# A decoder layer on one core: wider moving operands in up and query/key, an eleventh pair in down, another order at both ends

## The chip, the cores and the metric

The kernel runs on one core of one Trainium2 chip. The metric is the device time of one execution in microseconds; for the kernel before it is the median of three runs.

## What is computed

One decoder layer on x of 256 rows by 2048 columns, all in float32:

```python
h   = rmsnorm(x)                 # 2048 columns, gain
qkv = h @ w_in                   # 2048 x 6144: 16 heads of 128
# heads 0-7 stick-breaking attention, heads 8-15 rotary + dilated windows
mix = concat(head_rmsnorm(heads)) @ w_out
x   = x + rmsnorm(mix)
u   = causal_conv3(rmsnorm(x) @ w_up)        # 2048 x 11008
x   = x + rmsnorm((gelu(gate) * val) @ w_down)   # 5504 x 2048
```

## The kernel before

Matmuls run in fp32r. To keep float32's accuracy every operand is split in a high part (a copy, rounded) and a low part (the rest), and each product is three matmuls: high by high, high by low, low by high. A weight tile of 128 x 1024 (`raw`, 5 buffers, one DMA of 512 KB on SP's queue) becomes `wh` by ACT's cast (`high`, L86) and `wl` by DVE's subtraction (`low`, L91), 4 buffers each.

The work is a list of **chunks**, each one weight block of 2048 columns: 16 for the values (`v`), 32 for query and key (`qk`, one head's query or key each), 16 for the output projection (`out`), 86 for `up` (43 tiles of 128 gate columns, 43 of value columns, by turns). After each chunk the attention of some heads moves on by one step. In `v`, `out` and the down stage the weights are the moving operand, 512 columns at a time (`mm_moving`, L116 to L132). In `qk` and `up` the weights are stationary and the activations move, 256 columns (the sequence) at a time: `mm_stationary` (L94) multiplies each of the 16 blocks of `wh` with the high activations `hT0` (L100) and with the low ones `hT1` (L101), into the same 256 columns of PSUM, and then each block of `wl` with `hT0` (L104): 48 matmuls in a chunk. The first two up chunks go through `mm_stationary_late` (L106), which keeps that order of its own. `convolved` (L425) scales an up result by the row norm on DVE, straight from PSUM (L430), adds the three-tap convolution, and gives gate times value to `yt` or `yp`.

The **down stage** (class `Down`, L460) multiplies with w_down in two column halves (`cp` 0 and 1). Its 43 row tiles are units: a single ("one") has 4 products of 128x512; two tiles that form a pair take 7 products in place of 8, by sums of blocks (T13, T24 on DVE, L517 to L519; Rb, Ra). A pair needs four `wh` and four `wl`. `_down_plan` (L39) sets the order: 10 pairs with two singles behind each. `prepare` runs four units ahead of `multiply`. The sums T13 and T24 and the gain `gbc` lie in `spare`, the results in `fg`; `spare` takes the place of `hT1` and `fg` that of `hT0` after the last up chunk. `combine` (L540) and `close` (L550) bring the PSUM banks together when a half is done; `close` ends in a square sum on ACT, and in a gain product (`take`, L378) on DVE.

At the end of half 1 three singles are held back and multiplied bank by bank, first the banks of output rows 0 to 127, then those of rows 128 to 255, so that the norm of the first rows (`mean`, `newton`) and its four output steps (`put`, L577, and the output DMA) run beside the matmuls of the second. `put` scales, adds the residual and issues the DMA.

```python
T.matmul(ps, ws, hi[:, k, :], start=(k == 0), stop=False)      # L100
T.matmul(ps, ws, lo[:, k, :], start=False, stop=False)         # L101
...
spare = cpool.tile([P, 2 * D], F32, tag="hT1", name="spare")   # L762
```

A scheduler orders the instructions of each engine, apart from stretches marked to stay as written; each engine and each DMA queue then runs its list in order.

Of the kernel before, what the change touches and what calls it, by code (L numbers as in the profile page):

```python
# [33 lines left out]
NPAIR = 10  # L34
PAIRS = [(4 * m, 4 * m + 1) for m in range(NPAIR)]
# [14 lines left out]
def layer_kernel(ctx: ExitStack, tc: tile.TileContext, a, out: bass.AP):  # L50
# [135 lines left out]
    hT = [cpool.tile([P, KT, S], F32R, tag=f"hT{i}", name=f"hT{i}") for i in range(2)]  # L186
# [12 lines left out]
    def load_x(lo, hi):  # L199
        nc.sync.dma_start(xt[:, lo:hi, :], a["xT"][:, lo * S:hi * S].rearrange("p (k s) -> p k s", k=hi - lo))  # L200
# [27 lines left out]
    nc.scalar.dma_start(ident, a["cst"][:, C_ID:C_END])  # L228

    negones = cpool.tile([P, P], F32, name="negones")  # L230
# [102 lines left out]
    def dilated_head(h, ps):  # L333
        rot = apool.tile([P, 2, S], F32, tag="t2", name="rot", bufs=3)
        A.copy(rot[0:64], ps[64:128])
        A.copy(rot[64:128], ps[0:64])
        qk = apool.tile([P, 2, S], F32, tag="qk", name="qk", bufs=3)
        V.tensor_tensor(qk, ps, cosR, op=ALU.mult)
# [502 lines left out]
```

## Time and profile before

| | |
|---|---|
| median of 3 runs | 1142.37 us (1142.11 to 1142.76) |
| the profiled execution | 1142.97 us, of which the span is 1141.2 us |
| PE busy | 1119.8 us, 98% of the span, 7708 matmuls |
| DVE, ACT, POOL busy | 815.2, 625.8 and 2.0 us |
| the chain that ended last | 95% PE |
| granted TensorE clock | 0.998 of full |
| DMA | 217 MB, 190 GB/s on the mean |

The page gives each engine's busy time in the span, then the chain of work that ended last. An engine's busy share is an average over stages with different limits. For matmuls the recorded length is the latency of one; since they are pipelined, what one costs is the distance from its start to the next one's.

### The profile page before, as it was taken

The numbers are of one execution on the slowest core, as the hardware profiler recorded it, in microseconds if no ns is written. First come the engines' busy times: TensorE is split into PE (matmuls) and PEld (weight loads), VectorE is DVE, ScalarE is ACT, GpSimd is POOL, SyncE is SP. The second block draws the span as 40 slices with busy tenths as digits, with TensorE's granted clock in tenths as the row PEclk, the third lists the DMA queues.
The fourth block names the chain that finished last, engine by engine and source line by source line (L and its number), as shares of the span: only waits on it lengthen the run. The fifth ranks groups of instructions, "written<-read, shape, count | busy, mean of one in ns | idle before, by whom it ended". The sixth has DMA issues, their size and how long they took to land.

```text
span 1141.2 us, 19401 instructions
## 1 busy us (share of the span) xinstructions
PE 1119.8 (98%) x7708; PEld 1034.4 (91%) x7708; DVE 815.2 (71%) x1218; ACT 625.8 (55%) x919; POOL 2.0 (0%) x8
## 2 busy tenths in 40 slices
PE   7999999999999989999999999999999999999996
PEld 5998999989988889999999999999999988877884
DVE  6655565665655488777777777776777788898887
ACT  7555555555644376555555555555555555555653
POOL 0000000000000000000000000000000000000000
PEclk9999999999999999999999999999999999999999
DMA  9755545555545556555555555555555556645565
GB/s 341 268 197 166 180 153 166 167 163 173 167 164 187 182 192 201 186 188 185 187 186 187 184 187 184 190 185 184 186 185 185 185 191 216 207 161 205 206 199 184
DMA packets 60138, 217.08 MB, mean 190 GB/s; under 512 B 6800, under 2 KB 7696, under 8 KB 59280
## 3 DMA queue, kind: packets, MB, share of 16 engines
q1 hardware_dynamic: 59904, 215.78, 57.2%
q8 instruction: 60, 0.98, 0.3%
q14 instruction: 30, 0.25, 0.1%
q10 hardware_dynamic: 144, 0.07, 0.0%
HBM read 211.63 MB, written 4.19 MB: 189 GB/s over the span
## 4 chain that ended last, share of the span: by engine, by line
PE 95%; DVE 2%; ACT 1%; DMA 1%; issue 0%; DVEq 0%; SPq 0%; ACTq 0%
PE mmu L101 14%; PE mmu L104 14%; PE mmu L100 14%; PE p L536 6%; PE p L537 6%; PE p L535 6%; PE mmqk L100 5%; PE mmqk L104 5%; PE mmqk L101 5%; PE mmo L127 3%; PE mmo L130 3%; PE mmo L126 3%; PE mmv L126 2%; PE mmv L127 2%; PE mmv L130 2%; DMA mg<-in_xT 1%
## 5 line engine op out<-in xcount | busy, mean ns | idle before, releaser
L86 ACT CAST wh<-raw 128x1024 fp32r<-128x1024 f32 (+1 forms) x388 | 395.7, 1023 | 354.0 <-PE mmu L101 173.3
L91 DVE TENSOR_TENSOR wl<-raw,wh 128x1024 fp32r<-128x1024 f32 (+1 forms) x388 | 458.5, 1189 | 170.2 <-ACT wh L86 169.0
L100 PE MATMUL mmu<-hT,wh 128*128 128x256 f32 x1344 | 326.2, 281 | 0.2 <-ACT wh L86 0.2
L101 PE MATMUL mmu<-hT,wh 128*128 128x256 f32 x1344 | 325.8, 281 | 0.0
L100 PEld LDWEIGHTS mmu<-hT,wh 128*128 128x128 f32 x1344 | 253.9, 189 | 0.4 <-ACT wh L86 0.4
L101 PEld LDWEIGHTS mmu<-hT,wh 128*128 128x128 f32 x1344 | 252.6, 188 | 0.0
L104 PE MATMUL mmu<-hT,wl 128*128 128x256 f32 x1344 | 186.4, 281 | 0.0
L104 PEld LDWEIGHTS mmu<-hT,wl 128*128 128x128 f32 x1344 | 170.4, 188 | 0.0
L100 PE MATMUL mmqk<-hT,wh 128*128 128x256 f32 x512 | 126.8, 286 | 0.0
L101 PE MATMUL mmqk<-hT,wh 128*128 128x256 f32 x512 | 124.0, 281 | 0.0
L430 DVE TENSOR_TENSOR u<-mmu,r2B 128x256 f32<-128x256 f32 x86 | 36.4, 424 | 97.2 <-PE mmu L104 97.1
L101 PEld LDWEIGHTS mmqk<-hT,wh 128*128 128x128 f32 x512 | 96.6, 189 | 0.2
L100 PEld LDWEIGHTS mmqk<-hT,wh 128*128 128x128 f32 x512 | 96.4, 188 | 0.2
L86 ACT CAST wh<-spare 128x1024 fp32r<-128x1024 f32 x40 | 42.1, 1051 | 67.4 <-DVE spare L517 58.6
L536 PE MATMUL p<-wh,yt 128*128 128x512 f32 x184 | 73.4, 399 | 0.0
L535 PE MATMUL p<-wh,yt 128*128 128x512 f32 x184 | 72.5, 394 | 0.0
L537 PE MATMUL p<-wl,yt 128*128 128x512 f32 x184 | 71.8, 393 | 0.2 <-DVE wl L91 0.2
L104 PE MATMUL mmqk<-hT,wl 128*128 128x256 f32 x512 | 71.0, 281 | 0.0
L432 ACT ACTIVATE cv<-u,par 128x256 f32<-128x256 f32 x86 | 51.7, 602 | 27.6 <-DVE u L430 27.6
L104 PEld LDWEIGHTS mmqk<-hT,wl 128*128 128x128 f32 x512 | 65.1, 188 | 0.0
L126 PE MATMUL mmv<-wh,hT 128*128 128x512 f32 x128 | 52.6, 411 | 6.7 <-ACT hT L206 5.4
L536 PE MATMUL p<-wh,yp 128*128 128x512 f32 x140 | 55.8, 399 | 0.0
(165 smaller groups left out, 1343.6 us busy)
## 6 DMA issues: line engine op xcount, KB each, us to landing
raw<-in_w_up SPq DMA_DIRECT2D x172, 512.0 KB, 4.6
raw<-in_w_dn SPq DMA_DIRECT2D x86, 512.0 KB, 4.1
raw<-in_w_qk SPq DMA_DIRECT2D x64, 512.0 KB, 3.6
raw<-in_w_o SPq DMA_DIRECT2D x32, 512.0 KB, 3.6
raw<-in_w_v SPq DMA_DIRECT2D x30, 512.0 KB, 3.8
x<-in_x SPq DMA_DIRECT2D x2, 1024.0 KB, 8.8
x_kept<-x SPq DMA_DIRECT2D x2, 1024.0 KB, 4.1
x1b<-x_kept SPq DMA_DIRECT2D x4, 512.0 KB, 4.9
```

What stands on the lines that cost most here:

```text
L86: pin(A.copy(wh, raw))
L91: pin(V.tensor_tensor(wl, raw, wh.bitcast(F32), op=ALU.subtract))
L100: T.matmul(ps, ws, hi[:, k, :], start=(k == 0), stop=False)
L101: T.matmul(ps, ws, lo[:, k, :], start=False, stop=False)
L104: T.matmul(ps, wl[:, j * P:(j + 1) * P], hi[:, k, :], start=False, stop=(k == KT - 1))
L126: T.matmul(ps[t], hi[:, k, tc_], ws, start=(first and i == 0 and j == 0), stop=False)
L127: T.matmul(ps[t], lo[:, k, tc_], ws, start=False, stop=False)
L130: T.matmul(ps[t], hi[:, k, tc_], wl[:, j * 512:(j + 1) * 512], start=False, stop=(last and i == len(parts) - 1 and j == n - 1))
L432: A.activation(cv, u, AF.Identity, scale=cw(2), bias=par[:, P_CB + f:P_CB + f + 1])
L535: T.matmul(ps, hi, wh[:, cs], start=(cp, bank) not in self.begun, stop=False)
L536: T.matmul(ps, lo, wh[:, cs], start=False, stop=False)
L537: T.matmul(ps, hi, wl[:, cs], start=False, stop=self.left[cp, bank] == 0)
```

## The change

In `qk` and `up` the high and low activations now lie in one tile `hT2`, side by side for each block, and one matmul with 512 moving columns takes the place of L100 and L101; its two halves land side by side in one bank, and the low weights still take 256 columns (L104). The two halves are added afterwards: ACT copies one out of PSUM, DVE adds the other (`both` in up, the same two steps in qk, where the sum then lies in SBUF before the head's first step). The down stage forms 11 pairs and 21 singles in place of 10 and 23; singles are spread evenly between pairs, except that 4 remain for the end of each half. The gain products of half 0 are no longer run at the change of halves but one behind each of the first singles of half 1. `gbc` is multiplied by -0.5 once, and `take` becomes a plain product; three of the four of half 1, and half of the last, run on POOL. At the end the last bank is split in two halves of 256 columns, and the output steps have other widths. At the start the x tiles and the gain come through ACT's queue, eight matmuls on zeros run first, and the first chunk's weights come in three pieces in place of four. In `qk` and `first_norm`, tiles move between pools; the other edits not shown here give the same steps new operands.

```diff
-NPAIR = 10
-PAIRS = [(4 * m, 4 * m + 1) for m in range(NPAIR)]
+NPAIR = 11
+HELD = 4
+PAIRS = [(FT // NPAIR * m, FT // NPAIR * m + 1) for m in range(NPAIR)]
...
     plan = [("one", left.pop(0)) for _ in range(0 if cp else 2)]
+    spread = len(left) - HELD
     for m in range(NPAIR):
         plan.append(("pair", m))
-        plan += [("one", left.pop(0)) for _ in range(2 if cp or m < NPAIR - 1 else 0)]
+        plan += [("one", left.pop(0)) for _ in range((m + 1) * spread // NPAIR - m * spread // NPAIR)]
     return plan + [("one", k) for k in left]
...
-    def mm_stationary(ps, parts, hi, lo):
+    def mm_stationary(ps, parts, h):
...
-                ws = wh[:, j * P:(j + 1) * P]
-                T.matmul(ps, ws, hi[:, k, :], start=(k == 0), stop=False)
-                T.matmul(ps, ws, lo[:, k, :], start=False, stop=False)
+                T.matmul(ps, wh[:, j * P:(j + 1) * P], h[:, k, :, :], start=(k == 0), stop=False, skip_group_check=True)
             for j in range(8):
                 k = 8 * i + j
-                T.matmul(ps, wl[:, j * P:(j + 1) * P], hi[:, k, :], start=False, stop=(k == KT - 1))
+                T.matmul(ps[:, 0, :], wl[:, j * P:(j + 1) * P], h[:, k, 0, :], start=False, stop=(k == KT - 1), skip_group_check=True)
...
+    def both(ps, pool, name):
+
+        half = pool.tile([P, S], F32, tag="half", name="half", bufs=1)
+        A.copy(half, ps[:, 1, :])
+        u = pool.tile([P, S], F32, tag=name, name=name)
+        V.tensor_tensor(u, ps[:, 0, :], half, op=ALU.add)
+        return u
...
-    hT = [cpool.tile([P, KT, S], F32R, tag=f"hT{i}", name=f"hT{i}") for i in range(2)]
+    hT2 = cpool.tile([P, KT, 2, S], F32R, tag="hT", name="hT")
+    hT = [hT2[:, :, i, :] for i in range(2)]
...
-    for k in range(4):
-        raws[0] += load(chunks[0][3][:, k * 512:(k + 1) * 512], 512)
-        load_x(k, k + 1)
-        if k == 0:
-            nc.sync.dma_start(gpre, a["par"][:, P_PRE:P_PRE + KT])
-        split_x(k, k + 1)
-        parts_of[0] += split(raws[0][k:k + 1])
+    nc.scalar.dma_start(gpre, a["par"][:, P_PRE:P_PRE + KT])
+    warm = cpool.tile([P, 512], BF16, name="warm")
+    V.memset(warm, 0.0)
+    idle = ps_at.tile([P, 512], F32, tag="at", name="idle")
+    for _ in range(8):
+        T.matmul(idle, warm[:, 0:P], warm, start=True, stop=True)
+    for lo, hi in ((0, 1), (1, 2), (2, 4)):
+        raws[0] += load(chunks[0][3][:, lo * 512:hi * 512], (hi - lo) * 512)
+        load_x(lo, hi, nc.scalar)
...
+            split_x(lo, hi)
+            parts_of[0] += split(raws[0][-1:])
+    nc.scalar.dma_start(ident, a["cst"][:, C_ID:C_END])
...
-        u = phB.tile([P, S], F32, tag="u", name="u")
-        V.tensor_tensor(u, ps, r2B, op=ALU.mult)
+        u = both(ps, phB, "u")
+        V.tensor_tensor(u, u, r2B, op=ALU.mult)
...
-                        t13, t24 = spare[:, D:D + HALF], spare[:, D + HALF:]
+                        t13, t24 = room[:, 3, 0:HALF], room[:, 3, HALF:]
...
-            rows.squares(dst, t, col)
-            return lambda: rows.take(dst, t, col)
+            rows.squares(dst, t, col + (1 if lo else 0))
+            return lambda eng: eng.tensor_tensor(dst, dst, gbc[:, col * 512 + lo:col * 512 + hi], op=ALU.mult)
...
+                    if later and self.units[u][1] == "one":
+                        later.pop(0)(V)
                 if cp == 0:
-                    for b in (4, 3, 2, 8):
-                        self.close(0, b)()
-            u = 2 * n - 3
+                    later = [self.close(0, b) for b in (4, 3, 2, 8)]
+            u = 2 * n - HELD
...
+            for b in (2, 3):
+                products(b)
+                self.close(1, b)(G)
+            r = rows.newton(*rows.mean(0))
+            products(4)
+            put(0, 0, 1024, r)
+            take = self.close(1, 4)
+            put(0, 1024, 1536, r)
+            take(G)
+            products(8, 0, 256)
+            put(0, 1536, 2048, r)
+            self.close(1, 8, 0, 256)(G)
+            products(8, 256, 512)
+            take = self.close(1, 8, 256, 512)
+            mean = rows.mean(1, 5)
+            take(V)
+            r = rows.newton(*mean)
+            for lo, hi in ((0, 1024), (1024, 1472), (1472, 1856), (1856, 2048)):
+                put(1, lo, hi, r)
...
-    spare = cpool.tile([P, 2 * D], F32, tag="hT1", name="spare")
-    gbc = spare[:, 0:D]
+    room = cpool.tile([P, 4, D], F32, tag="hT", name="room")
+    fg, gbc = room[:, 0:2, :], room[:, 2, :]
     nc.sync.dma_start(gbc, a["gpost"][1:2, :].partition_broadcast(P))
-    fg = cpool.tile([P, 2, D], F32, tag="hT0", name="fg")
-    rows = Rows(fg, "d")
+    V.tensor_scalar(gbc, gbc, -0.5, None, op0=ALU.mult)
```

Where the change moves instructions, the lists of the engines show it (lines are those of either file, so L100 of before has no counterpart in the other). PE in half an up chunk, before; `mmu` is the PSUM tile, `hT_74` the high and `hT_75` the low activations, and four of the eight pairs of rows ahead of the row with `wl` are shown:

```order
L100 MATMUL mmu<-hT_74,wh 128x256
L101 MATMUL mmu<-hT_75,wh 128x256
L100 MATMUL mmu<-hT_74,wh 128x256
L101 MATMUL mmu<-hT_75,wh 128x256
L100 MATMUL mmu<-hT_74,wh 128x256
L101 MATMUL mmu<-hT_75,wh 128x256
L100 MATMUL mmu<-hT_74,wh 128x256
L101 MATMUL mmu<-hT_75,wh 128x256
L104 MATMUL mmu<-hT_74,wl 128x256 x8
```

and now, the last up chunk whole, and the first matmul of down:

```order
L101 MATMUL mmu<-hT,wh 128x512 x8
L104 MATMUL mmu<-hT,wl 128x256 x8
L101 MATMUL mmu<-hT,wh 128x512 x8
L104 MATMUL mmu<-hT,wl 128x256 x8
L555 MATMUL p_8866<-wh,yt_3925 128x512
```

Sixteen matmuls of 256 columns in each half chunk have become eight of 512, and the eight with `wl` are as they were.

DVE from the end of up into down, before; `spare` holds the sums T13 and T24, the first `wl<-raw` behind them is that of Rb:

```order
L517 TENSOR_TENSOR spare<-raw 128x1024
L430 TENSOR_TENSOR u<-mmu,r2B 128x256
L518 TENSOR_TENSOR spare<-spare,raw 128x512
L519 TENSOR_TENSOR spare<-spare,raw 128x512
L433 SCALAR_TENSOR_TENSOR cv<-u,par,cv 128x255
L91 TENSOR_TENSOR wl<-spare,wh 128x1024
L434 SCALAR_TENSOR_TENSOR cv<-u,par,cv 128x254
L91 TENSOR_TENSOR wl<-spare,wh 128x1024
L442 TENSOR_TENSOR cv<-cv 128x256
L91 TENSOR_TENSOR wl<-raw,wh 128x1024
```

and now (`room` holds the sums, the gain and the results):

```order
L536 TENSOR_TENSOR room<-raw 128x1024
L121 TENSOR_TENSOR u<-mmu,half 128x256
L537 TENSOR_TENSOR room<-room,raw 128x512
L447 TENSOR_TENSOR u<-u,r2B 128x256
L538 TENSOR_TENSOR room<-room,raw 128x512
L93 TENSOR_TENSOR wl<-room,wh 128x1024
L450 SCALAR_TENSOR_TENSOR cv<-u,par,cv 128x255
L93 TENSOR_TENSOR wl<-room,wh 128x1024
L451 SCALAR_TENSOR_TENSOR cv<-u,par,cv 128x254
L807 TENSOR_SCALAR room<-room 128x2048
L459 TENSOR_TENSOR cv<-cv 128x256
L93 TENSOR_TENSOR wl<-raw,wh 128x1024
```

An addition of the two halves (L121) and the scaling of the gain (L807, 2048 columns) stand ahead of the `wl` of Rb (the first `wl<-raw` here), which is the tenth row of the first list and the twelfth of the second.

DVE at the end of the program, before; L555 is `close`, L378 the gain product, L577 `put`:

```order
L555 TENSOR_TENSOR fg<-p_11232,fg 128x512
L395 SCALAR_TENSOR_TENSOR rs<-rq,rr 128x1
L577 SCALAR_TENSOR_TENSOR fg<-fg,rs,x1b 128x512 x4
L555 TENSOR_TENSOR fg<-p_11235,fg 128x512
L378 SCALAR_TENSOR_TENSOR fg<-fg,spare 128x512
L384 TENSOR_SCALAR rj,rv<-ssd 128x4
L378 SCALAR_TENSOR_TENSOR fg<-fg,spare 128x512
L393 SCALAR_TENSOR_TENSOR rq<-rr,rv 128x1
L395 SCALAR_TENSOR_TENSOR rs<-rq,rr 128x1
L577 SCALAR_TENSOR_TENSOR fg<-fg,rs,x1b 128x256
L577 SCALAR_TENSOR_TENSOR fg<-fg,rs,x1b 128x768
L577 SCALAR_TENSOR_TENSOR fg<-fg,rs,x1b 128x512 x2
```

and now, where L575 is `close`, L577 the gain product and L610 `put`:

```order
L575 TENSOR_TENSOR room<-p_9759,room 128x512
L401 TENSOR_SCALAR rj,rv<-ssd 128x4
L410 SCALAR_TENSOR_TENSOR rq<-rr,rv 128x1
L412 SCALAR_TENSOR_TENSOR rs<-rq,rr 128x1
L610 SCALAR_TENSOR_TENSOR room<-room,rs,x1b 128x1024
L575 TENSOR_TENSOR room<-p_9758,room 128x512
L610 SCALAR_TENSOR_TENSOR room<-room,rs,x1b 128x512 x2
L575 TENSOR_TENSOR room<-p_10561,room 128x256
L575 TENSOR_TENSOR room<-p_10562,room 128x256
L401 TENSOR_SCALAR rj,rv<-ssd 128x5
L577 TENSOR_TENSOR room<-room 128x256
L410 SCALAR_TENSOR_TENSOR rq<-rr,rv 128x1
```

Between the matmuls of the first rows and the last `close` stood four puts and two gain products; now three puts and no gain product stand there, and the last `close` has 256 columns.

## Rows read from the trace of the kernel before

**Rows 1.** The page, part 1 (busy us, share) and part 4 (the chain, by engine).

```profile
PE 1119.8 (98%) x7708; PEld 1034.4 (91%) x7708; DVE 815.2 (71%) x1218; ACT 625.8 (55%) x919; POOL 2.0 (0%) x8
...
PE 95%; DVE 2%; ACT 1%; DMA 1%; issue 0%; DVEq 0%; SPq 0%; ACTq 0%
```

**Rows 2.** Timeline, PE in an up chunk: start, length, engine, line, operation.

```profile
600.75 0.28 PE L100 MATMUL mmu<-hT,wh 128*128 128x256 f32 x1
...
603.59 0.28 PE L100 MATMUL mmu<-hT,wh 128*128 128x256 f32 x1
```

**Rows 3.** Timeline, PE in the down stage.

```profile
919.98 0.39 PE L535 MATMUL p<-wh,yp 128*128 128x512 f32 x1
...
920.68 0.39 PE L535 MATMUL p<-wh,yp 128*128 128x512 f32 x1
```

**Rows 4.** Busy time by stretch: length, PE, PEld, DVE, ACT, POOL, clock, DMA.

```profile
430.00:890.00 460.00, 460.00 (x3890) 460.00 (x3889) 341.47 (x531) 253.28 (x329) 0.00 (x0) 1.00 0.58 187
```

**Rows 5.** Groups by line, shapes apart: busy us, mean ns, idle before.

```profile
L430 DVE TENSOR_TENSOR u<-mmu,r2B 128x256 f32<-128x256 f32 x86 | 36.4, 424 | 97.2 <-PE mmu L104 97.1
...
L443 ACT CAST yt<-cv 128x256 fp32r<-128x256 f32 x23 | 9.4, 407 | 0.5
```

**Rows 6.** Timeline, the first 15 us, PE and ACT.

```profile
5.37 0.80 PE L126 MATMUL mmv<-wh,hT 128*128 128x512 f32 x1 [5.37 <-ACT hT L206]
...
9.12 0.39 PE L130 MATMUL mmv<-wl,hT 128*128 128x512 f32 x1
...
11.85 1.71 ACT L206 ACTIVATE hT<-mg,gpre 128x256 fp32r<-128x256 f32 x4 [0.83 <-DMA mg<-in_xT]
...
14.54 0.50 PE L126 MATMUL mmv<-wh,hT 128*128 128x512 f32 x1 [1.37 <-ACT wh L86]
```

**Rows 7.** Timeline, PE at the change of column halves.

```profile
1021.02 0.40 PE L536 MATMUL p<-wh,yt 128*128 128x512 f32 x1
1022.51 0.50 PE L537 MATMUL p<-wl,yp 128*128 128x512 f32 x1 [1.10 <-DVE wl L91]
...
1023.65 1.21 PE L537 MATMUL p<-wl,yt 128*128 128x512 f32 x4 [0.17 <-DVE wl L91]
```

**Rows 8.** Timeline, DVE in the middle of down, one pair and two singles.

```profile
995.23 1.23 DVE L91 TENSOR_TENSOR wl<-raw,wh 128x1024 fp32r<-128x1024 f32 x1 [0.18 <-ACT wh L86]
...
1004.33 1.23 DVE L91 TENSOR_TENSOR wl<-raw,wh 128x1024 fp32r<-128x1024 f32 x1 [1.09 <-ACT wh L86]
```

**Rows 9.** Timeline, from the last up chunk into down, DVE and PE.

```profile
901.04 1.23 DVE L517 TENSOR_TENSOR spare<-raw 128x1024 f32<-128x1024 f32 x1 [2.27 <-PE mmu L101]
901.79 0.39 PE L535 MATMUL p<-wh,yt 128*128 128x512 f32 x1
...
907.28 1.22 DVE L91 TENSOR_TENSOR wl<-raw,wh 128x1024 fp32r<-128x1024 f32 x1
```

**Rows 10.** Groups by line, DVE's scalings: busy us, mean ns.

```profile
L247 DVE TENSOR_SCALAR diag<-ident,rstd 128x128 f32<-128x128 f32 x2 | 0.6, 286 | 4.6 <-PE rps L248 4.6
...
L402 DVE TENSOR_SCALAR r2B<-r2ps 128x256 f32<-128x256 f32 x1 | 0.4, 417 | 0.0
```

**Rows 11.** DMA issues: KB each, median us to landing.

```profile
spare<-in_gpost SPq DMA_DIRECT2D x1, 1024.0 KB, 5.3
```

**Rows 12.** Timeline, the end, PE and DVE.

```profile
1126.58 0.69 DVE L555 TENSOR_TENSOR fg<-p,fg 128x512 f32<-128x512 f32 x1
...
1130.35 0.39 PE L537 MATMUL p<-wl,yt 128*128 128x512 f32 x1
...
1132.38 0.68 DVE L555 TENSOR_TENSOR fg<-p,fg 128x512 f32<-128x512 f32 x1
...
1135.04 2.74 DVE L577 SCALAR_TENSOR_TENSOR fg<-fg,rs,x1b 128x256 f32<-128x256 f32 x4
```

**Rows 13.** Timeline, POOL's two casts.

```profile
4.40 0.29 POOL L254 CAST idb<-ident 128x128 bf16<-128x128 f32 x1 [3.32 <-DMA ident<-in_cst]
34.26 1.15 POOL L255 CAST mskb<-cst 128x128 bf16<-128x128 f32 x1 [29.58 <-DMA cst<-in_cst]
```

More of the change, by code (lines that the diff above doesn't have):

```diff
@@ L227, in layer_kernel @@
     between[7] = (par, a["par"])
-    nc.scalar.dma_start(ident, a["cst"][:, C_ID:C_END])
-    negones = cpool.tile([P, P], F32, name="negones")
+    negones = apool.tile([P, P], F32, name="negones", bufs=1)
     G.memset(negones, -1.0)
@@ L331, in stick_head, with dilated_head @@
         yield from finish_head(h, at, None)
[L333 removed]
+    def dilated_head(h, qk):
         rot = apool.tile([P, 2, S], F32, tag="t2", name="rot", bufs=3)
[L335 to L338, printed above, removed]
+        A.copy(rot[0:64], qk[64:128])
+        A.copy(rot[64:128], qk[0:64])
+        V.tensor_tensor(qk, qk, cosR, op=ALU.mult)
         V.tensor_tensor(rot, rot, sinR, op=ALU.mult)
@@ L491, in __init__ @@
             self.left = {}
-            for u in self.units:
+            for i, u in enumerate(self.units):
                 for bank, _, _ in u[4]:
-                    self.left[u[0], bank] = self.left.get((u[0], bank), 0) + 1
+                    last = bank == 8 and i >= len(self.units) - HELD
+                    for key in ((1, 8, 0), (1, 8, 256)) if last else ((u[0], bank),):
+                        self.left[key] = self.left.get(key, 0) + 1
             self.begun = set()
@@ L569, in run @@
                         self.combine(cp)
+                    if later and self.units[u][1] == "one":
+                        later.pop(0)(V)
                 if cp == 0:
-                    for b in (4, 3, 2, 8):
-                        self.close(0, b)()
-            u = 2 * n - 3
+                    later = [self.close(0, b) for b in (4, 3, 2, 8)]
+            u = 2 * n - HELD
             self.prepare(2 * n)
-            def put(t, lo, hi, r):
-                V.scalar_tensor_tensor(fg[:, t, lo:hi], fg[:, t, lo:hi], r, x1s[2 * t + lo // HALF][:, lo % HALF:(hi - 1) % HALF + 1], op0=ALU.mult, op1=ALU.add)
-                nc.sync.dma_start(out[t * P:(t + 1) * P, lo:hi], fg[:, t, lo:hi])
+            held = range(u, 2 * n)
+            last = fg[:, 1, 1536:2048]
+            V.tensor_tensor(last, last, self.ps[8,], op=ALU.subtract)
+            self.ps |= {(8, lo): ps_at.tile([P, 256], F32, tag="at", name="p9") for lo in (0, 256)}
             x1s = []
@@ L583, in run, with put, products @@
                 nc.sync.dma_start(x1s[h], x1_kept[h // 2 * P:(h // 2 + 1) * P, h % 2 * HALF:(h % 2 + 1) * HALF])
-            for t, banks in ((0, (2, 3)), (1, (4, 8))):
-                takes = []
-                for b in banks:
-                    for v in range(u, 2 * n):
-                        self.multiply(v, [x for x in self.ONE if x[0] == b])
-                    takes.append(self.close(1, b))
-                vr = rows.mean(t)
-                for take in takes:
-                    take()
-                r = rows.newton(*vr)
-                cuts = (0, 512, 1024, 1536, 2048) if t == 0 else (0, 256, 1024, 1536, 2048)
-                for lo, hi in zip(cuts, cuts[1:]):
-                    put(t, lo, hi, r)
+            def put(t, lo, hi, r):
+                x = x1s[2 * t + lo // HALF][:, lo % HALF:(hi - 1) % HALF + 1]
+                V.scalar_tensor_tensor(fg[:, t, lo:hi], fg[:, t, lo:hi], r, x, op0=ALU.mult, op1=ALU.add)
+                nc.sync.dma_start(out[t * P:(t + 1) * P, lo:hi], fg[:, t, lo:hi])
+            def products(bank, lo=0, hi=512):
+                for v in held:
+                    self.multiply(v, [x for x in self.ONE if x[0] == bank], lo, hi)
+            for b in (2, 3):
[17 more added lines that the diff above has]
+                put(1, lo, hi, r)
     down = Down()
@@ L751, in layer_kernel @@
                 held.append((ps, parts))
-                mm_stationary_late(held, hT[0], hT[1])
+                mm_stationary_late(held, hT2)
                 pinned[0] = True
```

90 lines of the change are left out of this document (51 added, 39 removed).

## The prediction

> **What bounds it now.** I read the page's totals and the chain first: PE is busy 98% of the span and makes 95% of the chain that ended last [rows 1]. So a term counts only where it shortens the matmul stream, opens or closes a gap in it, or changes what lies ahead of its first or behind its last matmul. The page's lengths of matmuls are latencies; the timeline gives what one costs, from start to start. In an up chunk 24 matmuls of 256 columns take 603.59 - 600.75 = 2.84 us, 0.1183 each [rows 2]. In down, three of 512 columns take 0.70 us, 0.2333 each [rows 3]. The next views are of places where PE doesn't run at that pace, the start, the change of column halves, the way into down, the tail, and of the engines that get more work.
>
> The sum is made against the profiled execution, 1142.97 us, which is 0.6 above the median of the three runs, 1142.37. About 0.2% (2.3 us) is what a measurement of this kernel can tell from no change.
>
> **512 columns in up and query/key.** Two matmuls of 256 cost 0.2367, one of 512 costs 0.2333: 3.3 ns saved. Each of 116 chunks (32 qk, 86 up less the first two, which keep their own order) has 16 such mergers: 1856 x 3.33 ns = **-6.2 us**. Of this the two spacings are measured, but no row shows 512 columns moved out of hT; that is a rival below.
> The Trainium skill, "TensorE: Matmul & The Clock Gate", section "Back-to-back issue gap", puts a constant 2.5 ns on each matmul beside its columns, so that a merger would save 2.5 ns and the term be -4.6 us by estimate; the rows here show 233.3 and 236.7, and the trace has the last word.
>
> Added are, per chunk, a copy of 128x256 on ACT and an addition of 128x256 on DVE. From 430 to 890 us DVE is busy 341.47 of 460 us and ACT 253.28, while PE never pauses [rows 4]. The nearest rows of the new steps are 0.42 us on DVE and 0.41 on ACT [rows 5]. With 0.42 per 5.63 us DVE goes from 74% to 82% and ACT from 55% to 62%. PE covers both: I count nothing. Without that cover the addition alone would be 116 x 0.42 = 49 us. DVE's wait in front of L430 is for the chunk's last matmul [rows 5], so it stands ready there, not late.
>
> **The eleventh pair.** Two singles are 8 products, a pair 7; a product has three matmuls, and there are two halves: 972 matmuls become 966, 6 x 0.2333 = **-1.4 us**. What its sums and casts cost DVE is weighed in rival 2.
>
> **The start.** From 5.37 to 9.12 PE makes eight steps in 3.75 us where the pace after it gives 1.87 [rows 6]; most are 0.43 long, the spacing of 512 columns at the lower of TensorE's two levels, 1.2 GHz. Matmuls on zeros that run ahead can give back at most 1.9 us. But the first chunk's 24 matmuls end near 13 us and the next chunk starts at 14.54 behind ACT, whose four casts of hT began at 11.85 upon a DMA and took 1.71 [rows 6]. What PE gains before this point is lost in the wait, unless that DMA lands earlier. The x tiles now have a queue of their own, so the first ones can; but the third transfer is issued behind two casts on ACT, and the first matmul now waits for a product and a subtraction on DVE. Bounds -1.9 and +2.0; I take **-0.7**, the part that I expect the earlier first transfers to carry through to the second chunk. ident is issued later on ACT's queue; what it feeds is used by the first attention step, chunks later: nothing.
>
> **The change of halves.** Between 1021.02 and 1023.65 PE issues 4 matmuls, 0.93 us at its pace, in 2.63: two waits for a `wl` of DVE [rows 7]. DVE is late there because the gain products of half 0 and the closing additions stand ahead of these subtractions. The products move behind the singles of half 1, and six singles instead of two lie around the change, which take less DVE time for each matmul than pairs. The whole gap goes: **-1.7 us**; bounds 0 (the closing additions remain) and -1.7. The moved products, 4 of 0.7 us, fall where DVE waits 1.1 us for ACT in each period [rows 8]: nothing.
>
> **The way into down.** PE's first matmul of down starts at 901.79; `wl` of Rb, which the first pair's last products need, ends on DVE at 907.28 + 1.22 = 908.50 [rows 9]. PE needs it 38 matmuls in, at 901.79 + 38 x 0.2333 = 910.66: 2.16 us of slack. Now more stands ahead of it. T13 must wait for the last matmul that reads hT2, no longer for the last one with the low activations, which was done at 901.04 [rows 9]: 0.9 us later. The addition of the last tile's halves adds 0.34 net of what became cheaper. Then the scaling of gbc by -0.5: 2048 columns on DVE. Scalings of 128 and 256 columns took 286 and 417 ns [rows 10], 1.02 ns for each further column: 0.286 + 1920 x 1.02 ns = 2.25 us. Together 3.5: Rb is late by 1.3, and DVE, now with less lead, runs out once more in the first pair and its one single, some 0.6: **+1.9 us**. Bounds: nothing, if that scaling runs at half the price, and +3.0 if no lead is left for the pair behind it. gbc's transfer takes 5.3 us to land [rows 11]; issued at 902 it is there at 907.3, about when DVE comes to it, so it isn't what is late. It holds SP's queue until hT2 is free, 0.9 us longer than `spare` did; five `raw` buffers cover that.
> Of this scaling the Trainium skill, "VectorE: DVE Perf Modes", section "The perf-mode tier table (the rule you actually need)", states 1227 ns for 2048 columns of float32 in SBUF. By that the stall would be 1.0 us smaller and the time 1131.8; the row of 128 columns, all in SBUF, doesn't look like the faster mode, and I stay with the rows.
>
> **The tail.** Let M be the start of the last matmul, 1130.35 [rows 12]. Before, the last `close` starts 2.03 us behind M, held up by four puts; its square, gain products and norm follow, the last four puts (2.74) start at M + 4.69, and the span ends at M + 10.85. Now DVE has three puts ahead: the `close` of the second bank (0.69, as at 1126.58) ends 4.5 us ahead of M, since 12 matmuls of 512 and 24 of 256 columns follow it on PE (5.6 us); the puts of 1024, 512 and 512 end 0.7 after M, and the two halves of the last `close` (0.42 each) end at M + 1.4. One square of 256 columns, the norm and the last half's product follow: the puts start at M + 3.15 and, if the span ends 6.2 us behind that as before, it ends at M + 9.3. **-1.5 us**; bounds -2.2 (nothing at all waits for DVE) and +1.8 (the rival on POOL).
>
> **Held singles.** Four `wh`, `wl` must be ready ahead of the held stretch in place of three; the buffers are four, and the last one's are ready 2.4 us after a unit is freed where PE takes 2.6. Nothing.
>
> **Sum**: -6.2 - 1.4 - 0.7 - 1.7 + 1.9 - 1.5 = -9.6. 1142.97 - 9.6 = 1133.4 for such an execution, **1132.8 us** for the median.
>
> **The rivals.**
> 1. POOL is slow. Three products of 512 columns and one of 256 move to it. Its only rows are two casts of 128x128, 0.29 and 1.15 us [rows 13]; four times as many columns make 1.2 to 4.6. At 1.2 each is done well ahead of its put. At 4.6 the four run one behind the other from M - 7.3 and end at M - 2.7, + 1.9, + 6.5 and + 8.8; the last put of rows 128 to 255 then ends near M + 9.8 and the span at M + 12.6: the tail costs +1.8 in place of -1.5, **1136.1**. It decides from about 3 us a product on, where the fourth ends behind M + 3.15. Chance 13%.
> The Trainium skill, "GPSIMD Engine Reference", section "2.1 Instruction dispatch", tells of a load of code at the first call of a routine; that would be the same rival, at its first product, and no run here shows it yet.
> 2. The slower side: DVE becomes the bound in down. A period of a pair and two singles is about 10.5 us; in it DVE waits 0.18 + 1.09 = 1.27 us for ACT's casts [rows 8] and works 9.2. With 11 pairs a period is shorter: 15 singles among 11 pairs in half 0, 17 in half 1, with PE times of 8.7 and 9.2 and DVE work of 8.45 and 8.7. Were those 1.27 us tied to DVE's own order, each period would be 1.0 or 0.7 longer than PE's: 11 x 1.72 = +18.9, **1151.7**. It turns the sign from about 0.85 us of wait in each period on. Against it: ACT is late there because it waits for PE to give back a `wh`, so the wait is slack of a stream bound by PE and shrinks with the period. Chance 4%.
> 3. 512 columns out of hT cost as much as twice 256, or DVE and ACT's added steps take back the 6.2: **1139.0**. Chance 7%. For it: no row moves 512 columns there; against it: 233 ns in down with float32 weights of the same size.
> 4. Start and way into down both at their worse bounds: +2.7 and +1.1 more, **1136.6**. Chance 6%.
>
> **Numbers.** The forecast, 1129.5 to 1135.0, has 70%; rivals 1 to 4 have 13, 4, 7 and 6%. The range reaches down for the lower bounds of the tail, the start and the way into down (-0.7 - 1.2 - 1.9, of which I don't expect all) and up over rivals 1 and 4: 1129.5 to 1138.0. Rival 3 and 2 lie outside, and some of what I haven't seen. Faster needs less than 1140.1, which all but rival 2 give: 95%; within 0.2% 1%, slower 4%.
>
> **What would show it.** In an up chunk, L101 starts 0.233 apart, L104 0.118, a chunk 5.63 us with no gap of PE. In down 965 steps; a wait of PE for `wl` of Rb 1 to 2 us long within the first 45 matmuls, behind a scaling of 2.2 us on DVE; no gap at the change of halves; the last `close` within 1.5 us of the last matmul; POOL's products 1.2 us each. Wrong it would be with pauses of PE in every pair of down (rival 2), with L101 at 0.237 (rival 3), or with the last puts waiting for POOL (rival 1).

## The result, and the profile after

The changed kernel takes **1135.21 us** (median of 4 runs, 1134.44 to 1135.26), the one before 1142.57 (1142.11 to 1143.09): ratio 0.9934, 95% interval 0.9917 to 0.9951. Forecast were 1132.8 and 1129.5 to 1138.0. The time lies in the range, but not for the reasons given: the largest term of the sum came out, most of the others didn't, and some 6 us of shorter steps that no term named stand beside a loss that only a rival named. So the number held in part by luck.

The profiled executions are 1142.97 and 1135.25 us. The page after, parts 1 and 4 (before: [rows 1]):

```profile
PE 1113.1 (98%) x5866; PEld 944.1 (83%) x5866; DVE 864.1 (76%) x1350; ACT 647.1 (57%) x1041; POOL 6.1 (1%) x12
...
PE 94%; DVE 2%; ACT 1%; DMA 1%; issue 0%; DVEq 0%; SPq 0%; ACTq 0%
```

PE bounds it as before. Where the time went is read from PE's timeline at the borders of the stages. Before: the first matmul of query/key and of the output projection, and the first transpose behind the projection:

```profile
31.44 0.28 PE L100 MATMUL mmqk<-hT,wh 128*128 128x256 f32 x1
...
311.35 0.48 PE L126 MATMUL mmo<-wh,mix 128*128 128x512 f32 x1
...
403.82 1.04 PE L667 MATMUL pth<-ident,x 128*128 128x128 f32 x8
```

After, the same three, the first matmul of down and the last one of all (before: 901.79 in [rows 9], 1130.35 in [rows 12]):

```profile
33.14 2.02 PE L101 MATMUL mmqk<-hT,wh 128*128 128x512 f32 x8
...
311.43 0.47 PE L134 MATMUL mmo<-wh,mix 128*128 128x512 f32 x1
...
402.25 1.03 PE L709 MATMUL pth<-ident,x 128*128 128x128 f32 x8
...
895.62 0.39 PE L555 MATMUL p<-wh,yt 128*128 128x512 f32 x1
...
1122.99 0.28 PE L557 MATMUL p<-wl,yt 128*128 128x256 f32 x1
```

| stretch | before | after | difference | forecast |
|---|---|---|---|---|
| up to query/key | 31.44 | 33.14 | +1.70 | -0.7 |
| query/key (and values) | 279.91 | 278.29 | -1.62 | -1.7 |
| output projection | 92.47 | 90.82 | -1.65 | 0 |
| norm and up | 497.97 | 493.37 | -4.60 | -4.5 |
| down, to the last matmul | 228.56 | 227.37 | -1.19 | -1.2 |
| behind it, to the span's end | 10.8 | 10.2 | -0.65 | -1.5 |
| outside the span | 1.8 | 2.1 | +0.3 | 0 |

**512 columns.** PE in half an up chunk, after:

```profile
600.22 2.02 PE L101 MATMUL mmu<-hT,wh 128*128 128x512 f32 x8
602.08 1.11 PE L104 MATMUL mmu<-hT,wl 128*128 128x256 f32 x8
603.04 2.02 PE L101 MATMUL mmu<-hT,wh 128*128 128x512 f32 x8
```

Half a chunk now takes 2.82 us where it took 2.84 [rows 2] (2.813 and 2.840 in the median), 16 matmuls in place of 24: the term of -6.2 came out as -1.62 - 4.60.

**Output projection.** Nothing was changed there, 384 matmuls of 512 columns stand in the same order, and it is 1.65 us shorter: 4.3 ns for each matmul. In down the step fell from 0.2333 [rows 3] to about 0.229 too, as these two rows, thirty steps apart, show:

```profile
1053.42 0.39 PE L555 MATMUL p<-wh,yp 128*128 128x512 f32 x1
...
1060.30 0.39 PE L555 MATMUL p<-wh,yt 128*128 128x512 f32 x1
```

That makes 954 x 4.4 ns = 4.2 us (the other 24 of its 978 matmuls have 256 columns). Yet down won 1.19 in all. With -1.4 for the eleventh pair, PE must wait some 4.4 us more in it than before.

**Down.** What PE's clearly longer steps exceed the usual one by adds up to some 6 us in the trace, where it was 2.0; these are the waits that are given for down from here on. The view of PE's waits names a part, since many are shorter than it counts:

```profile
PE p L557 <- DVE wl L93: 1.9, 5, 0.6
PE p L555 <- ACT wh L88: 0.3, 1, 0.3
```

No gap is left at the change of halves ([rows 7] had 1.70 us). Busy time after, in two stretches of down (columns as in [rows 4]):

```profile
906.00:1010.00 104.00, 103.22 (x444) 82.41 (x443) 99.06 (x104) 58.14 (x65) 0.00 (x0) 1.00 0.59 207
1010.00:1112.00 102.00, 100.50 (x432) 80.28 (x432) 92.62 (x98) 58.03 (x70) 0.00 (x0) 1.00 0.59 204
```

DVE is busy 95% and 91%: hardly a microsecond in ten to catch up. In the timeline of after, T13 of a pair waits 2.07 us for its weight tile, and PE then waits for the `wl` behind it:

```profile
1060.38 1.23 DVE L536 TENSOR_TENSOR room<-raw 128x1024 f32<-128x1024 f32 x1 [2.07 <-DMA raw<-in_w_dn]
...
1064.25 0.50 PE L557 MATMUL p<-wl,yp 128*128 128x512 f32 x1 [0.59 <-DVE wl L93]
```

So not all of this is work of DVE: between 905 and 1110 us, T13 waits 7.2 us in all for weight tiles, where it waited 3.1 before. Late tiles alone don't make PE wait, though: in a run with ten pairs (e10, below) T13 waits 7.1 us for them, and PE 0.6 in the whole of down.

The way into down costs less than I said. The scaling of `gbc` and the `wl` of Rb, timeline after:

```profile
901.90 1.22 DVE L807 TENSOR_SCALAR room<-room 128x2048 f32<-128x2048 f32 x1
...
903.37 1.22 DVE L93 TENSOR_TENSOR wl<-raw,wh 128x1024 fp32r<-128x1024 f32 x1
```

The scaling took 1.22 us, not 2.25: here the Trainium skill ("VectorE: DVE Perf Modes", "The perf-mode tier table (the rule you actually need)", 1227 ns) was right, and my row of 128 columns misled. `wl` of Rb is there at 904.6, 0.3 after PE's 38th step; PE loses 0.9 us at the pair behind it and 0.3 at the next.

**The start.** After:

```profile
1.19 3.60 PE L225 MATMUL idle<-warm 128*128 128x512 bf16 x8 [1.19 <-DVE warm L222]
...
7.05 0.35 DVE L230 TENSOR_SCALAR hT<-mg,gpre 128x256 fp32r<-128x256 f32 x1
...
7.55 0.71 PE L134 MATMUL mmv<-wh,hT 128*128 128x512 f32 x2 [2.76 <-DVE hT L230]
...
11.38 0.63 PE L138 MATMUL mmv<-wl,hT 128*128 128x512 f32 x1
...
12.97 0.50 PE L134 MATMUL mmv<-wh,hT 128*128 128x512 f32 x1 [0.96 <-ACT hT L215]
```

and the stretches (the clock is the third number from the end):

```profile
5.80:9.20 3.40, 1.65 (x7) 1.19 (x7) 1.67 (x4) 1.39 (x3) 0.00 (x0) 0.95 0.98 352
9.20:12.60 3.40, 2.81 (x7) 1.56 (x6) 1.48 (x2) 0.86 (x2) 0.00 (x0) 0.54 1.00 397
```

The zeros end at 4.8, but the first product of x now stands on DVE behind two subtractions, the second of which waits for its weight piece, and the first real matmul comes at 7.55 where it came at 5.37 [rows 6]. TensorE idled 2.76 us in between and is granted 0.54 of full speed from 9.2 to 12.6, which is the lower level, so the slow steps are still there, only later.

Neither of the two sets the loss, though. The last of the 12 matmuls of the first two weight pieces starts at 11.38 us, and the 13th, the first of the third piece (the row at 12.97), waits for ACT, which waits for the third transfer of x. (Only the first three of its six transfers, four tiles of 16, go through ACT's queue; the others stay on SP's.) These are rows of ACT, and the first matmul of the second chunk:

```profile
5.80 0.34 ACTq L209 DMA_DIRECT2D mg<-in_xT  x1
...
12.41 2.51 ACT L215 ACTIVATE hT<-mg,gpre 128x256 fp32r<-128x256 f32 x6 [2.54 <-DMA mg<-in_xT]
...
16.17 0.39 PE L134 MATMUL mmv<-wh,hT 128*128 128x512 f32 x1
```

That transfer is issued behind two casts on ACT, at 5.80, and lands 6.6 us later; before, the transfers of these x tiles were issued on SP's queue up to 5.0 us, and the 13th matmul started at 10.05. Six products of hT instead of four then stand ahead of the second chunk's casts on ACT, and that chunk starts at 16.17 where it started at 14.54 [rows 6]: +1.63 of the 1.70.

**The tail**, after:

```profile
1122.66 1.41 DVE L610 SCALAR_TENSOR_TENSOR room<-room,rs,x1b 128x512 f32<-128x512 f32 x2
...
1123.58 2.29 POOL L577 TENSOR_TENSOR room<-room 128x512 f32<-128x512 f32 x2 [2.96 <-ACT jks L391]
1123.98 0.75 DVE L575 TENSOR_TENSOR room<-p,room 128x256 f32<-128x256 f32 x2
...
1126.70 2.74 DVE L610 SCALAR_TENSOR_TENSOR room<-room,rs,x1b 128x1024 f32<-128x1024 f32 x4
```

POOL's first two products take 1.29 each, the first no longer than the second; the row at 1123.58 holds the third and the one of 256 columns, 2.29 together; they hold nobody (rival 1 is out). The last puts start at M + 3.71 where I had M + 3.15 (M is the start of the last matmul, 1122.99): both halves of the last `close` wait for two puts to end, and their two squares on ACT run one behind the other.

### The profile page after: what moved, and what is told of

Its sections match the earlier page's. It is cut to its first block, busy times and chain, and to the rows that moved or that the text cites. A ratio compares the mean times of both kernels' runs of the same rounds, so it can differ in the third digit from the quotient of the medians.

```text
span 1133.2 us, 16046 instructions
## 1 busy us (share of the span) xinstructions
PE 1113.1 (98%) x5866; PEld 944.1 (83%) x5866; DVE 864.1 (76%) x1350; ACT 647.1 (57%) x1041; POOL 6.1 (1%) x12
## 4 chain that ended last, share of the span: by engine, by line
PE 94%; DVE 2%; ACT 1%; DMA 1%; issue 0%; DVEq 0%; SPq 0%; ACTq 0%
PE mmu L101 28%; PE mmu L104 14%; PE mmqk L101 11%; PE p L557 6%; PE p L555 6%; PE p L556 6%; PE mmqk L104 5%; PE mmo L138 3%; PE mmo L134 3%; PE mmv L135 3%; PE mmv L134 3%; PE mmo L135 3%; PE mmv L138 3%; DVE wl L93 1%; DMA mg<-in_xT 1%; PE mmu L111 1%
## 5 line engine op out<-in xcount | busy, mean ns | idle before, releaser
L101 PE MATMUL mmu<-hT,wh 128*128 128x512 f32 x1344 | 340.6, 395 | 0.2 <-ACT wh L88 0.2
L101 PEld LDWEIGHTS mmu<-hT,wh 128*128 128x128 f32 x1344 | 240.8, 188 | 44.9 <-ACT wh L88 0.4
L104 PEld LDWEIGHTS mmu<-hT,wl 128*128 128x128 f32 x1344 | 184.1, 188 | 15.3
L104 PE MATMUL mmu<-hT,wl 128*128 128x256 f32 x1344 | 187.4, 282 | 0.0
L101 PE MATMUL mmqk<-hT,wh 128*128 128x512 f32 x512 | 132.8, 400 | 0.0
L101 PEld LDWEIGHTS mmqk<-hT,wh 128*128 128x128 f32 x512 | 91.9, 188 | 17.0
L104 PEld LDWEIGHTS mmqk<-hT,wl 128*128 128x128 f32 x512 | 70.0, 188 | 5.8
L104 PE MATMUL mmqk<-hT,wl 128*128 128x256 f32 x512 | 71.2, 281 | 0.0
L557 PE MATMUL p<-wl,yt 128*128 128x512 f32 (+1 forms) x172 | 66.7, 389 | 0.2 <-DVE wl L93 0.2
L555 PE MATMUL p<-wh,yt 128*128 128x512 f32 (+1 forms) x172 | 66.5, 387 | 0.0
L556 PE MATMUL p<-wh,yt 128*128 128x512 f32 (+1 forms) x172 | 66.4, 386 | 0.0
L557 PE MATMUL p<-wl,yp 128*128 128x512 f32 x154 | 60.7, 399 | 1.7 <-DVE wl L93 1.7
L555 PE MATMUL p<-wh,yp 128*128 128x512 f32 x154 | 60.7, 394 | 0.4 <-ACT wh L88 0.3
L556 PE MATMUL p<-wh,yp 128*128 128x512 f32 x154 | 60.4, 392 | 0.0
L93 DVE TENSOR_TENSOR wl<-room,wh 128x1024 fp32r<-128x1024 f32 x44 | 53.7, 1221 | 5.6 <-ACT wh L88 4.8
L134 PE MATMUL mmv<-wh,hT 128*128 128x512 f32 x128 | 52.1, 409 | 3.7 <-DVE hT L230 2.8
L135 PE MATMUL mmv<-wh,hT 128*128 128x512 f32 x128 | 51.3, 401 | 0.0
```

The costliest lines, as they stand in the source:

```text
L93: pin(V.tensor_tensor(wl, raw, wh.bitcast(F32), op=ALU.subtract))
L101: T.matmul(ps, wh[:, j * P:(j + 1) * P], h[:, k, :, :], start=(k == 0), stop=False, skip_group_check=True)
L104: T.matmul(ps[:, 0, :], wl[:, j * P:(j + 1) * P], h[:, k, 0, :], start=False, stop=(k == KT - 1), skip_group_check=True)
L134: T.matmul(ps[t], hi[:, k, tc_], ws, start=(first and i == 0 and j == 0), stop=False)
L135: T.matmul(ps[t], lo[:, k, tc_], ws, start=False, stop=False)
L555: T.matmul(ps, yh, wh[:, cs], start=key not in self.begun, stop=False)
```

## The experiments

Medians are held against 1135.21; the kernel before, run along each time, had 1142.74 to 1142.81. What is read from one profiled execution is marked so.

**Theory.** The place of a tile in its partition sets the step of a matmul. The tile of the last norm's square sums grew from 32 to 40 bytes (`Rows(fg, "d", 5)`, an edit that isn't among those shown) and takes 32 bytes more in the layout. All tiles of the pools behind it moved with that, and mix, yt and yp came from 32 bytes off a multiple of 64 to a multiple of 64. (The tiles that changed pools, and `warm`, shift them by 512 bytes, which doesn't change this.) hT stayed 32 off, and the values, which have it as stationary operand, kept 0.2333. Rival: the order or the clock.

```diff
     small = ctx.enter_context(tc.tile_pool(name="small", bufs=4))
+    small.tile([P, 8], F32, tag="shift", name="shift", bufs=1)
```

In the changed kernel:

> The changed kernel with one unused tile of 32 bytes a partition ahead of the stages' pools, so that mix, yt and yp lie 32 bytes off a multiple of 64 again, as before the change; nothing else differs. Theory (the place of the stationary operand sets the step of a matmul): matmuls of the output projection and of down step at 0.2333 us again in place of 0.2288; the output projection takes 92.5 us again (+1.65), down loses 4.3 us of pace and wins back a part of its 5.95 us of stalls: 1138 to 1141 us. Rival (the changed order or the clock made these steps shorter): 1135.2 us, steps of 0.2288.

Measured: 1138.26 us (1136.89 to 1138.69). Its output projection, profiled:

```profile
311.55 0.48 PE L135 MATMUL mmo<-wh,mix 128*128 128x512 f32 x1
...
403.96 1.03 PE L710 MATMUL pth<-ident,x 128*128 128x128 f32 x8
```

92.41 us again, and down takes 227.96 us at steps of 0.2333, with some 2.7 us of waits. The same line in the kernel before:

> The kernel before with the same unused tile, so that mix, yt and yp come to lie on multiples of 64 bytes; nothing else differs. Theory (place): 384 matmuls of the output projection and 972 of down step at 0.2288: -1.7 and -4.4, less new stalls where DVE can't follow, 0 to 4 us: 1136.3 to 1140.3 us. Rival (order or clock): 1142.4 us, steps of 0.2333.

Measured: 1137.58 us (1137.34 to 1139.05), ratio to before 0.9956 (0.9944 to 0.9969). Its output projection:

```profile
311.42 0.47 PE L127 MATMUL mmo<-wh,mix 128*128 128x512 f32 x1
...
402.24 1.03 PE L668 MATMUL pth<-ident,x 128*128 128x128 f32 x8
```

90.82 us, and down 224.43 (900.18 to 1124.61). Place is shown, from both sides: an unused tile of 32 bytes gives the kernel before 5.2 us, about as much as all written parts of the change together (4.6 against the kernel before that ran along, by e1).

```diff
+    cpool.tile([P, 8], F32, name="shift0")
     hT2 = cpool.tile([P, KT, 2, S], F32R, tag="hT", name="hT")
+    cpool.tile([P, 8], F32, name="shift1")
```

> The changed kernel with 32 unused bytes ahead of hT2 and 32 behind it, so that hT2 lies on a multiple of 64 bytes too. Theory (place of the stationary operand): only the 384 matmuls of the values, where hT2 is stationary, step at 0.2288: -1.7 us, 1133.5. Theory extended (place of either operand): the 1856 matmuls of 512 columns that move hT2 gain 4.5 ns each too, -8.4 us, and those of 256 up to as much: 1117 to 1125. Rival (order or clock): 1135.2.

Measured: **1125.66** us (1124.86 to 1125.79). In the values, where hT2 is the stationary operand, the step is 0.229 now, nineteen of them in 4.35 us:

```profile
84.59 0.39 PE L134 MATMUL mmv<-wh,hT 128*128 128x512 f32 x1
...
88.94 0.39 PE L135 MATMUL mmv<-wh,hT 128*128 128x512 f32 x1
```

Here hT2 alone has another place, since the 64 bytes leave every tile behind it where it was to a multiple of 64. Where the rest is won neither form of the theory had; PE in half an up chunk:

```profile
600.33 2.02 PE L101 MATMUL mmu<-hT,wh 128*128 128x512 f32 x8
602.19 1.07 PE L104 MATMUL mmu<-hT,wl 128*128 128x256 f32 x8
603.10 2.02 PE L101 MATMUL mmu<-hT,wh 128*128 128x512 f32 x8
```

The eight of 512 still take 1.86 us, the eight of 256 take 0.91 in place of 0.96. Is that the place alone, or the 512s beside them? The same kernel with `L101` split in two of 256 (this variant no longer computes the layer, so only its times say something; number and size of all else are the same):

```diff
-                T.matmul(ps, wh[:, j * P:(j + 1) * P], h[:, k, :, :], start=(k == 0), ...)
+                for i2 in range(2):
+                    T.matmul(ps[:, i2, :], wh[:, j * P:(j + 1) * P], h[:, k, i2, :], start=(k == 0), ...)
```

> The kernel of e3_hT_shifted with each matmul of 512 columns in up and query/key split in two of 256 again, into the two halves of the same bank (ACT's copy and DVE's addition stay). Theory (what the wider operand is worth hangs on the place of hT2: on a multiple of 64 bytes a matmul of 256 takes 0.1145, two 0.2290, and one of 512 still takes 0.2327 there): 1856 x 3.7 ns = 6.9 us faster than e3's 1125.7: 1118.8. Rival (0.1145 was that of the 256s beside those of 512; alone they take 0.1183 again): 1125.7 + 1856 x 3.9 ns + 3712... of the others at most 6.9 = 1132 to 1140. Rival (both are the same): 1125.7.

Measured: 1134.11 us (1134.07 to 1134.54):

```profile
601.87 2.05 PE L102 MATMUL mmu<-hT,wh 128*128 128x256 f32 x16
603.75 1.10 PE L105 MATMUL mmu<-hT,wl 128*128 128x256 f32 x8
604.69 1.58 PE L102 MATMUL mmu<-hT,wh 128*128 128x256 f32 x12
```

In this chunk all 24 step at 0.1175, and so they do in all of up behind its first chunks. But in query/key of the same execution, 36 of the 64 half chunks, all of 256 columns too, step at 0.1133:

```profile
36.51 1.98 PE L102 MATMUL mmqk<-hT,wh 128*128 128x256 f32 x16
...
39.23 1.98 PE L102 MATMUL mmqk<-hT,wh 128*128 128x256 f32 x16
```

So 256s among themselves can have the whole gain of the place as well; in the kernel before, with hT 32 bytes off, no half chunk steps below 0.118. What decides between 0.1133 and 0.1178 isn't shown. The wider operand is worth 8.45 us here, more than the 6.2 without the shift, but by stages 9.0 us of it lie in norm and up (495.50 against 486.53) and 0.2 in query/key (275.77 against 275.57): with hT2 on a multiple of 64 its worth is mostly that up stays at the slower of the two steps without it.

**The start.** The start of before put back:

```diff
-    nc.scalar.dma_start(gpre, a["par"][:, P_PRE:P_PRE + KT])
...
-    for lo, hi in ((0, 1), (1, 2), (2, 4)):
...
+    for k in range(4):
+        raws[0] += load(chunks[0][3][:, k * 512:(k + 1) * 512], 512)
+        load_x(k, k + 1)
+        if k == 0:
+            nc.sync.dma_start(gpre, a["par"][:, P_PRE:P_PRE + KT])
+        split_x(k, k + 1)
+        parts_of[0] += split(raws[0][k:k + 1])
```

> The changed kernel with the start of before: four weight pieces, x on SP's queue, the gain behind the first x tile, no matmuls on zeros, ident last. My reading of the trace (the new start costs 1.70 us: the first matmul of query/key comes at 33.14 in place of 31.44): 1133.5 us, that matmul at 31.4 again. Rival (what the start loses the wait for the second chunk's data would cost anyway): 1135.2, 33.1.

Measured: 1131.49 us (1131.24 to 1131.78), the first matmul of query/key at 30.92: -2.2 at the start, and down took 1.6 less in the profiled execution, with 4.5 us of waits in place of 5.9; why that is so stays open. With the x transfers back on SP's queue the second chunk starts at 14.02. Nine matmuls on zeros ahead of that start:

```diff
+    for _ in range(9):
+        T.matmul(idle, warm[:, 0:P], warm, start=True, stop=True)
```

> The start of before (as in e4_old_start) with nine matmuls on zeros ahead of it. Theory (zeros help where real matmuls follow them at once; the slow steps of the first 3.7 us go, but the second chunk still waits for its data): 1130.0 to 1131.5, against 1131.5 of e4. Rival (all of the slow steps' cost comes back): 1129.6. Rival (nothing comes back): 1131.5.

Measured: 1132.94 us (1131.83 to 1134.7). PE, profiled:

```profile
11.54 0.39 PE L138 MATMUL mmv<-wl,hT 128*128 128x512 f32 x1
...
14.27 0.51 PE L134 MATMUL mmv<-wh,hT 128*128 128x512 f32 x1 [2.34 <-ACT wh L88]
```

The first chunk now ends 1 us sooner, and the second waits that much longer for its weights: nothing comes back. The median is even 1.45 us above e4's and outside the theory's range; why isn't shown.

**Down.** The two additions of T24 on POOL:

```diff
-                        V.tensor_tensor(t24[:, 0:512], t13[:, 0:512], rb[:, 512:], op=ALU.add)
-                        V.tensor_tensor(t24[:, 512:], t24[:, 0:512], ra[:, 512:], op=ALU.add)
+                        G.tensor_tensor(t24[:, 0:512], t13[:, 0:512], rb[:, 512:], op=ALU.add)
+                        G.tensor_tensor(t24[:, 512:], t24[:, 0:512], ra[:, 512:], op=ALU.add)
```

> The changed kernel with the two additions that make T24 (128x512 each) on POOL in place of DVE, in all 22 pairs. Theory (in down PE now waits because DVE has hardly time to spare: 192 of 206 us between 906 and 1112): DVE gets 1.38 us a pair back, PE's waits for wl in down fall from 5.9 us to about 1.5: 1130.5 to 1132. Rival (the waits come from weight tiles that land late): no change, 1135.2. A second rival (DVE and POOL hinder one another, or T24 comes too late with 1.29 us for each addition): 1137 or more.

Measured: 1169.86 us. The second rival, and far beyond my price; groups by line, and the view of waits in down:

```profile
L538 POOL TENSOR_TENSOR room<-room,raw 128x512 f32<-128x512 f32 x22 | 46.6, 2118 | 1.7
L537 POOL TENSOR_TENSOR room<-room,raw 128x512 f32<-128x512 f32 x22 | 36.4, 1654 | 1016.6 <-DVE room L536 1005.1 <-issue 9.0 <-DVE wl L93 2.6
```

```profile
ACT wh L88 <- POOL room L538: 59.1, 21, 3.4
ACT wh L88 <- DVE room L536: 47.2, 19, 4.3
```

An addition takes 1.65 to 2.12 us on POOL beside DVE, 0.69 on DVE; ACT's cast waits for it, and DVE, which has its subtractions in a fixed order, waits for the cast (37.8 us in all). What late weight tiles add to PE's waits, the first rival, this run can't tell.

```diff
-NPAIR = 11
+NPAIR = 10
```

> The changed kernel with 10 pairs and 23 singles, spread by the same rule. By the prediction's term alone (six matmuls less are worth 1.4 us): 1136.6. Theory (DVE is what PE waits for in down): two pairs fewer, one in each half, take 10 us from DVE, PE's waits fall from 5.9 us by 1.5 to 4, and against 6 more matmuls the time is 1132.5 to 1135.

Measured: 1133.87 us (1132.41 to 1134.6), though its profiled start was 1.5 us later (query/key at 34.68). Down took 225.47 us in place of 227.37, with 6 matmuls more and 2.9 us of waits: the theory's side, but the intervals overlap (0.9907 to 0.9934 against 0.9917 to 0.9951), and the profiled execution is the slowest of the four.

```diff
-    V.tensor_scalar(gbc, gbc, -0.5, None, op0=ALU.mult)
+    G.tensor_scalar(gbc, gbc, -0.5, None, op0=ALU.mult)
```

> The changed kernel with the scaling of gbc by -0.5 on POOL in place of DVE. Theory (the scaling, 1.22 us on DVE, is part of what stalls PE 0.9 us at the first pair and 0.3 at the next): 1134.2 to 1134.9. Rival (the later T13 and the addition of the halves make that stall): 1135.2.

Measured: 1138.00 us (1137.72 to 1138.92), worse than both. Timeline:

```profile
900.29 6.15 POOL L807 TENSOR_SCALAR room<-room 128x2048 f32<-128x2048 f32 x1 [865.39 <-DMA room<-in_gpost]
901.12 3.87 DVE L451 SCALAR_TENSOR_TENSOR cv<-u,par,cv 128x254 f32<-128x254 f32 x1
```

DVE's step of 0.48 us takes 3.87 while POOL works. The Trainium skill ("SBUF — State Buffer", "SBUF: two separate sides") says that the two engines share a pair of ports that one of them holds for a whole instruction. The trace agrees in that DVE is stopped, but not in the whole instruction: DVE goes on at 904.9, and its next subtraction takes its usual 1.21 us, while POOL's scaling is recorded up to 906.4 (ends on POOL are rough).

```diff
-                    later = [self.close(0, b) for b in (4, 3, 2, 8)]
+                    for b in (4, 3, 2, 8):
+                        self.close(0, b)(V)
```

> The changed kernel with the four gain products of half 0 at the change of halves again, directly behind each close; nothing else differs. By the prediction's term (a gap of 1.7 to 2.0 us at the change comes back): 1136.9. Rival (six singles around the change give DVE enough lead, the products there cost PE nothing): 1135.2. Rival (each product behind a single of half 1 costs PE a part of the stalls there, so it goes faster): 1133.5 to 1135.

Measured: 1135.53 us (1134.87 to 1136.57): no difference, with one wait of 0.38 us at the change in the profiled execution. With the products back at the change the gap stays closed, and e2, which has the old order, still has it (waits of 1.3 and 0.3 us). So the new order of pairs and singles is enough to close it, the moved products aren't needed.

**The parts that came out well together**: hT2 moved as in e3, the start of e4, ten pairs, and

```diff
-    V.tensor_scalar(gbc, gbc, -0.5, None, op0=ALU.mult)
+    A.activation(gbc, gbc, AF.Copy, scale=-0.5)
```

> The parts that came out well together: the changed kernel with hT2 on a multiple of 64 bytes (e3), the start of before (e4), ten pairs (e6), and the scaling of gbc on ACT in place of DVE. If the gains add (-9.6, -3.7, -1.3, and up to -0.9 for the scaling): 1119.7 to 1121.5. Rival (the stalls in down that e4 and e6 took away are the same ones, 1.4 of the 3.7 and the 1.3): 1121 to 1123.

Measured: **1120.16** us (1118.49 to 1121.22), ratio to before 0.9801 (0.9788 to 0.9814): faster than both kernels, by 22.6 and 15 us, as the sum of the gains had it. PE's waits in down add up to 0.6 us in the profiled execution. With eleven pairs:

```diff
-NPAIR = 10
+NPAIR = 11
```

> The kernel of e10_best_parts with eleven pairs again; nothing else differs. By the prediction's term (six matmuls less): 1118.8. Theory (at these steps DVE can't keep up with eleven pairs, and PE's waits in down rise from 0.6 us by more than the 1.4 they save): 1121.0 to 1124, with PE's waits in down at 3 to 5.5 us.

Measured: 1120.92 us (1120.07 to 1121.62). The profiled execution has the 4.3 us of waits that the theory wanted, so the eleventh pair does bring PE's waits. Yet the medians are 0.8 apart and the ranges overlap, and what was profiled is the slowest of this kernel's five executions and the fastest of e10's four. Which of ten and eleven is better isn't settled; that the eleventh brings 1.4 us is not seen in either pair of runs.

## Why the prediction was right in its number, and where it wasn't

- **512 columns** (-6.2): right in mechanism and size, -6.22 (not the -4.6 of the estimate beside it), with hT 32 bytes off a multiple of 64 as it was before; rival 3 is out. The added steps on ACT and DVE cost nothing, as forecast. How much it is worth hangs on hT's place (e3, e9), which I didn't know of.
- **The start** (-0.7): wrong, +1.70, though within its bounds. The failed step is that earlier first transfers would carry through to the second chunk. I named what failed, the third transfer behind two casts on ACT, and gave it no more than a bound of +2.0: it lands at 12.4, the 13th matmul waits for it, and the second chunk starts 1.63 us later. The first matmul is 2.2 us late as well, and the clock is lost again in the pause, but both are over before that wait ends. e8 shows that the slow steps had nothing to give back, as the wait at 14.54 in [rows 6] said.
- **The change of halves** (-1.7): the gap went, but it didn't need the moved products (e12).
- **The way into down** (+1.9): 1.2. The scaling was mis-sized, 1.22 us for 2.25. In e10 and e11, where ACT does it, 0.4 is left.
- **The eleventh pair** (-1.4) and **rival 2**: the six matmuls are gone, and DVE's waits came in their place. I held rival 2 at 4% by the old step of 0.2333. At that step eleven pairs (e1) have 2.7 us of waits in all, and ten pairs at 0.229 (e2) 2.2; with both, PE runs ahead of DVE and they are 6. The mechanism was real, at less than a quarter of the price.
- **The tail** (-1.5): -0.65, by two squares where I counted one, puts that ended 0.4 us later than I had them, and a span that ends 6.5 us behind the start of the last puts where I had 6.2.
- **What no step had**: mix, yt and yp came to another place, -1.65 in the output projection and -4.2 of steps in down, of which 3.05 us are left in the median (e1). Without it the time is 1138.26, 0.3 above my range. So the number held by luck: an unseen gain paid for a start, a tail and a DVE that I had priced too low.

## What to carry to other kernels

When a change adds, moves or resizes tiles, be it by a few bytes, compare the byte addresses of the operands of matmuls before and after, and hold a stage that wasn't edited against itself: its step tells whether the layout moved time. A faster PE brings the engine that feeds it nearer to being the bound, so a term that loads DVE has to be weighed at the new pace. Matmuls on zeros brought nothing here, neither with a pause of 2.76 us behind them nor with real ones at once behind them (e8), because data that came later set the time; so look first for the wait that ends last.

## What wasn't expected of the hardware

A stationary tile 32 bytes off a multiple of 64 makes a matmul of 512 columns step at 0.2333 us in place of 0.229 (e1, e2: 1.6 us in 384 matmuls; e3 in the values). With the moving hT2 on a multiple of 64, matmuls of 256 columns between ones of 512 step at 0.114 in place of 0.119 (e3); among themselves they step at 0.1133 in some stretches and at 0.1178 in others of one execution (e9). Only these two places were tried, and why they differ isn't shown. Work on POOL beside DVE is dear: a scaling of 2048 columns took 6.15 us on POOL and stretched a step of DVE from 0.48 to 3.87 (e7), and additions of 512 columns took 1.65 to 2.12 us on POOL in down (e5) where its first products of that size at the end, with DVE mostly idle, took 1.29.
